# A hybrid attention / state-space block on one Trainium2 core: the first k tile of the normed input lies 384 bytes off and is multiplied first, and small tiles are placed further ahead

## The chip, the core and the metric

The kernel runs on one core of a Trainium2 chip. Its time is the device time of one execution in microseconds (us). TensorE (PE) multiplies matrices, with its weight loads shown apart (PEld); VectorE (DVE) and ScalarE (ACT) do the elementwise work, GpSimd (POOL) a little of it, and the SyncE queue (SP) issues the loads of the weights.

## The reference

Two layers (`DEPTH = 2`) over 256 tokens of width 1024, all in float32; what matters here is that nearly every step multiplies 256 tokens by a large weight matrix:

```python
for l in range(DEPTH):
    h = rms_norm(x, norm_mix_w[l])
    proj = h @ w_in                      # 1024 -> 9320 columns: q, k, v, index, z, xbc, dt, gates
    a = dsa_attention(q, k, v, qi, ki, wi)       # top-64 attention, two blocks of 128 queries
    b = mamba2_branch(z, xbc, dt, ...)           # causal conv, chunked scan, gated group norm
    x = x + (sigmoid(g_attn) * (a @ w_proj_attn) + sigmoid(g_ssd) * (b @ w_proj_ssd)) @ w_out
    h = rms_norm(x, norm_ffn_w[l])
    u = causal_dwconv(h @ w_up)                  # 1024 -> 2 * 2816
    x = x + (silu(u[:, :2816]) * u[:, 2816:]) @ w_down
return rms_norm(x, norm_final_w)
```

## The kernel before

**Products in three parts.** Each float32 operand is split into a high part (rounded to fp32r) and a low part (what is left). A product is summed from high x high, high x low and low x high, so each 128x128 weight tile costs three matmuls with 256 columns (the tokens). Activations lie feature-major: k tile `k` is `[128, 256]`, 1024 bytes per partition.

**Chunks.** Weights come in chunks of 512 KB (eight 128x128 tiles) through a ring of five `raw` tiles. `take()` hands out the next chunk: ScalarE casts it to `whi` (L199), VectorE subtracts to `wlo` (L200), three such pairs deep. Some chunks are split early, into activation tiles that are free for a while (names that begin with `e`: `es0`, `ez0`, `ex0`, ...); their loads go through the same ring and queues.

**Loops.** `n_outer` makes one output tile of 128 features from one to three chunks: in each chunk `feed_high` goes over the eight k tiles with high x high (L376) and high x low (L377), and `feed_low` then goes over them again with `wlo` (L382): 24 matmuls. `k_outer` keeps four output tiles open and goes over k outside, also 24 matmuls for each chunk. `wide` (L548, L551, L554) has the activation as stationary and the weights as moving operand, with 308 or 512 columns.

**Who reads what, for each layer.** The scaled normed input `hxh`/`hxl` (made by `Normed.scaled`) feeds 56 `n_outer` chunks in the mixer (24 of the convolved columns, 16 gates, 16 `z`) and 36 in the FFN's up projection. `aH`/`aL` (attention) feed 8, `bH`/`bL` (scan) 8 in `k_outer` and 8 in `n_outer`, `mH`/`mL` (merged) 4 and 4, and the unscaled parts `uh`/`ul` the first 8 of the FFN and all of `wide`. `fH`/`fL` (FFN hidden, 22 k tiles) feed 11 chunks in `k_outer` and 12 in `n_outer`: 528 matmuls a layer, of which 192 read the tiles `fH0`, `fL0`, `fH1`, `fL1`.

**Side work.** Attention, scan and norms run as generators that `take()` steps on, so small matmuls of theirs stand between, and inside, the chunks. The framework's scheduler sets each engine's final order; engines run their own in order.

**Places.** Tiles of a pool lie one behind another in the order in which they are first made; a tile with a tag takes over that tag's place. Counted modulo 512 bytes within a partition, as built: all `whi`/`wlo` 64; `hxh`, `hxl`, `mH`, `mL`, `aH`, `aL`, `fH2` to `fH5` and their low parts 0; `bH`, `fH0`, `fH1`, `fL0`, `fL1` 384; `bL`, `uh`, `ul` 64. One weight tile is 512 bytes per partition and one k tile 1024, so all tiles of an array share its figure.

Of the kernel before, what the change touches and what calls it, by code (L numbers as in the profile page):

```python
# [63 lines left out]
def hybrid_kernel(ctx: ExitStack, tc: tile.TileContext, a: dict, out: bass.AP):  # L64
# [104 lines left out]
    def load_some(until=None):  # L169
        while st["dma"] < len(order) and st["dma"] < (until or st["prep"] + RAW_BUFS):  # L170
# [132 lines left out]
    class Normed:  # L303


        def __init__(self, nw, split=True):
            self.nw = nw
            self.acc = tmp.tile([P, T], F32, name="ssq", tag="ssq", bufs=3)
            if split:
                self.h = [act.tile([P, 4, T], F32R, name=f"uh{i}", tag=t) for i, t in enumerate(("Bm", "Cm"))]  # L310
                self.l = [act.tile([P, 4, T], F32R, name=f"ul{i}", tag=t) for i, t in enumerate(("lg0", "lg1"))]
            else:
                self.xw = act.tile([P, KD, T], F32, name="xw", tag="hxh")
            self.split = split

        def hi(self, k):
# [28 lines left out]
                nc.scalar.activation(self.xw[:, k, :], x, AF.Copy, scale=self.nw[:, k:k + 1])  # L345

        def scaled(self):
            h = act.tile([P, KD, T], F32R, name="hxh", tag="hxh")
            l = act.tile([P, KD, T], F32R, name="hxl", tag="hxl")
            for k in range(KD):  # L350
                t = tmp.tile([P, T], F32, name="ht", tag="ct", bufs=3)
                nc.vector.scalar_tensor_tensor(t, xT[:, k, :], self.nw[:, k:k + 1], self.row, op0=OP.mult, op1=OP.mult)
                nc.scalar.copy(out=h[:, k, :], in_=t)
                nc.vector.tensor_sub(l[:, k, :], t, h[:, k, :].bitcast(F32))
            return (lambda k: h[:, k, :]), (lambda k: l[:, k, :])

        def factor(self):
            ps = pst("sb", [P, 2], 2)
# [37 lines left out]
    def n_outer(parts):  # L396

        ps = acc_tile()
        for i, (hi, lo, ks) in enumerate(parts):
            wh, wl = take()  # L400
            feed_high(ps, wh, hi, lo, ks, i == 0)
            feed_low(ps, wl, hi, ks, i == len(parts) - 1)
        return ps


    nrm = Normed(sm("nmw", 0))
    side("norm", nrm.factor(), KD + 1)

    for l in range(L):

        tok = [act.tile([P, 8 * T], F32, name=f"big{t}", tag=f"big{t}")[:, :1856] for t in range(2)]
        V = [act.tile([P, T], F32, name=f"V{t}", tag=f"V{t}") for t in range(2)]
        wd = act.tile([P, 2, 40], F32, name="wd", tag="wd")

        def rotate(v, t, heads, dim, rot, o):
            h = rot // 2
# [17 lines left out]
        def index_stage():  # L434

            for t in range(2):
                s = slice(t * P, (t + 1) * P)
                rotate(tok[t][:, 0:576], t, 9, 64, 16, 64)
                kd = tmp.tile([P, 2, 64], F32, name="kd", tag="kd", bufs=1)
                nc.vector.tensor_copy(kd, tok[t][:, 512:576][:, None, :].to_broadcast([P, 2, 64]))  # L440
                yield 1
                ps = pst("sa", [P, 4, P], 2)
                for i in range(4):
                    nc.tensor.transpose(ps[:, i, :], tok[t][:, i * P:(i + 1) * P], ident)
                nc.scalar.copy(out=qiT[:, :, s], in_=ps)
                ps = pst("sa", [P, P], 2)
                nc.tensor.transpose(ps, kd.rearrange("p a b -> p (a b)"), ident)
                nc.scalar.copy(out=kiT[:, s], in_=ps)
            for b in range(2):
                yield 1  # L450
                yield from choose(b)
# [48 lines left out]
        dA = act.tile([P, 2, 32], F32, name="dA", tag="dA")  # L500
        Pc = act.tile([P, 2, 32], F32, name="Pc", tag="Pc")
        nP = act.tile([P, 2, 32], F32, name="nP", tag="nP")
        dec = act.tile([P, 32], F32, name="dec", tag="dec")

        prd = dram.tile([32, 2, P], F32, name=f"prd{l}")

        def decay_stage():
            def f64(tag):
                return tmp.tile([P, 2, 32], F32, name=tag, tag=tag, bufs=1)

            xd, u, z, z2, pl = f64("xd"), f64("u"), f64("z"), f64("z2"), f64("pl")
            ea = tmp.tile([P, 32], F32, name="ea", tag="ea", bufs=1)
            nc.scalar.activation(ea, sm("alog", l), AF.Exp)
            nc.vector.tensor_add(xd, wd[:, :, 8:40], sm("dtb", l)[:, None, :].to_broadcast([P, 2, 32]))
            nc.vector.scalar_tensor_tensor(u, xd, -1.0, xd, op0=OP.mult, op1=OP.min)
            nc.scalar.activation(u, u, AF.Exp)
            nc.vector.tensor_scalar(z, u, 2.0, None, op0=OP.add)
            nc.vector.reciprocal(z, z)
            nc.vector.tensor_mul(z, z, u)
            nc.vector.tensor_mul(z2, z, z)  # L520
            nc.vector.tensor_scalar(pl, z2, 2.0 / 17, None, op0=OP.mult)
            for n in range(15, 1, -2):
                nc.vector.scalar_tensor_tensor(pl, pl, 2.0 / n, z2, op0=OP.add, op1=OP.mult)
# [310 lines left out]
            gate_and_project(n)  # L834


        mH = act.tile([P, KD, T], F32R, name="mH", tag="hxh")
        mL = act.tile([P, KD, T], F32R, name="mL", tag="hxl")
        bh = lambda k: bH[k // 4][:, k % 4, :]
        bl = lambda k: bL[k // 4][:, k % 4, :]  # L840
        def merge(n, ps):
# [78 lines left out]


    finish("norm")
    y = act.tile([P, 2, 2, 512], F32, name="y", tag="hxl")
    for c in range(2):
        for h in range(2):
            ps = pst("acc", [P, 512], 4)
# [93 lines left out]
```

## Time and profile before

| | |
|---|---|
| time, median of 3 runs (lowest to highest) | 1068.74 us (1068.19 to 1072.17) |
| profiled execution: its time, its span | 1067.94 us, 1066.1 us |
| PE busy | 1056.1 us, 99% of the span, 8713 matmuls |
| PEld busy | 1020.8 us, 96% |
| DVE, ACT, POOL busy | 860.7 us (81%), 694.8 us (65%), 81.4 us (8%) |
| HBM read | 189.26 MB, 179 GB/s over the span |

PE's busy time covers the span because matmuls overlap: one takes some 280 ns from its start to its end, and the next begins after 113 to 118 ns. So the busy share says nothing of how close together they come. That is read from the times at which matmuls start.

### The profile page before, as it was taken

The numbers are of one execution on the slowest core, as the hardware profiler recorded it, in microseconds if no ns is written. First come the engines' busy times: TensorE is split into PE (matmuls) and PEld (weight loads), VectorE is DVE, ScalarE is ACT, GpSimd is POOL, SyncE is SP. The second block draws the span as 40 slices with busy tenths as digits, with TensorE's granted clock in tenths as the row PEclk, the third lists the DMA queues.
The fourth block names the chain that finished last, engine by engine and source line by source line (L and its number), as shares of the span: only waits on it lengthen the run. The fifth ranks groups of instructions, "written<-read, shape, count | busy, mean of one in ns | idle before, by whom it ended". The sixth has DMA issues, their size and how long they took to land.

```text
span 1066.1 us, 22377 instructions
## 1 busy us (share of the span) xinstructions
PE 1056.1 (99%) x8713; PEld 1020.8 (96%) x8713; DVE 860.7 (81%) x1652; ACT 694.8 (65%) x1285; POOL 81.4 (8%) x88
## 2 busy tenths in 40 slices
PE   9999999999999999999999999999999999999997
PEld 8799999999999999999997999899999999999997
DVE  6999979789677898886577999887895878988643
ACT  6769878567555566665465789775674556666552
POOL 3000000033001000000100000000420020000011
PEclk9999999999999999999999999999999999999999
DMA  8655445555677256667645654554666761666661
GB/s 309 208 185 191 141 140 179 148 181 176 201 235 247 80 159 197 195 194 240 195 134 167 220 159 139 168 168 146 179 183 207 259 218 42 195 197 195 185 184 51
DMA packets 53688, 191.81 MB, mean 180 GB/s; under 512 B 6176, under 2 KB 7216, under 8 KB 52560
## 3 DMA queue, kind: packets, MB, share of 16 engines
q1 hardware_dynamic: 51840, 180.71, 54.5%
q0 software_dynamic: 1600, 9.69, 2.4%
q8 instruction: 68, 1.11, 0.4%
q14 instruction: 36, 0.29, 0.1%
q10 hardware_dynamic: 144, 0.01, 0.0%
HBM read 189.26 MB, written 1.11 MB: 179 GB/s over the span
## 4 chain that ended last, share of the span: by engine, by line
PE 87%; DMA 6%; DVE 3%; issue 1%; ACT 1%; POOL 0%; SPq 0%; POOLq 0%; DVEq 0%; ACTq 0%
PE acc L376 22%; PE acc L377 22%; PE acc L382 22%; DMA raw<-in_wu_dram 5%; PE acc L548 3%; PE acc L551 3%; PE acc L554 3%; PE sa L377 2%; PE sa L376 2%; PE sa L382 2%; PE sb L731 2%; DVE ul L330 1%; PE sa L615 1%; PE sa L640 1%; DVE wlo L200 1%
## 5 line engine op out<-in xcount | busy, mean ns | idle before, releaser
L199 ACT CAST whi<-raw 128x1024 fp32r<-128x1024 f32 (+2 forms) x320 | 332.0, 1040 | 225.2 <-PE acc L377 137.0
L200 DVE TENSOR_TENSOR wlo<-raw,whi 128x1024 fp32r<-128x1024 f32 (+2 forms) x320 | 386.5, 1210 | 102.1 <-ACT whi L199 95.4
L376 PE MATMUL acc<-hxh,whi 128*128 128x256 f32 x1456 | 352.3, 282 | 0.0
L377 PE MATMUL acc<-hxl,whi 128*128 128x256 f32 x1456 | 349.7, 280 | 0.0
L377 PEld LDWEIGHTS acc<-hxl,whi 128*128 128x128 f32 x1456 | 274.3, 188 | 1.8 <-issue 1.6
L376 PEld LDWEIGHTS acc<-hxh,whi 128*128 128x128 f32 x1456 | 274.3, 188 | 1.5 <-issue 1.2
L382 PE MATMUL acc<-hxh,wlo 128*128 128x256 f32 x1456 | 200.6, 279 | 0.0
L382 PEld LDWEIGHTS acc<-hxh,wlo 128*128 128x128 f32 x1456 | 182.0, 188 | 0.6 <-issue 0.5
L675 DVE SCALAR_TENSOR_TENSOR cv<-acc,half,cv 128x255 f32<-128x255 f32 (+2 forms) x144 | 66.6, 472 | 4.1 <-ACT cv L673 3.7
L877 DVE SCALAR_TENSOR_TENSOR cv<-acc,small,cv 128x255 f32<-128x255 f32 (+1 forms) x144 | 68.5, 477 | 1.3
L343 POOL TENSOR_TENSOR ssq<-ssq,sq 128x256 f32<-128x256 f32 x30 | 27.8, 928 | 498.4 <-ACT sq L339 495.1
L376 PE MATMUL acc<-fH,whi 128*128 128x256 f32 x264 | 64.0, 277 | 0.0
L377 PE MATMUL acc<-fL,whi 128*128 128x256 f32 x264 | 63.9, 277 | 0.0
L377 PEld LDWEIGHTS acc<-fL,whi 128*128 128x128 f32 x264 | 49.6, 188 | 0.0
L376 PEld LDWEIGHTS acc<-fH,whi 128*128 128x128 f32 x264 | 49.5, 188 | 0.0
L377 PE MATMUL acc<-bL,whi 128*128 128x256 f32 x192 | 47.6, 282 | 0.0
L376 PE MATMUL acc<-bH,whi 128*128 128x256 f32 x192 | 47.5, 279 | 0.0
L721 ACT ACTIVATE bc<-bc,nP 128x128 f32<-128x128 f32 x128 | 40.5, 392 | 7.5 <-DMA bc<-prd 7.4
L830 POOL TENSOR_TENSOR ssq<-ssq,sq 128x256 f32<-128x256 f32 x24 | 32.2, 1343 | 136.5 <-ACT sq L829 136.1
L875 ACT ACTIVATE cv<-acc,small 128x256 f32<-128x256 f32 x72 | 40.6, 563 | 0.1
L382 PE MATMUL acc<-fH,wlo 128*128 128x256 f32 x264 | 37.8, 277 | 0.0
L377 PEld LDWEIGHTS acc<-bL,whi 128*128 128x128 f32 x192 | 36.2, 188 | 0.0
(346 smaller groups left out, 2011.4 us busy)
## 6 DMA issues: line engine op xcount, KB each, us to landing
raw<-in_wu_dram SPq DMA_DIRECT2D x88, 512.0 KB, 4.0
raw<-in_wx_dram SPq DMA_DIRECT2D x48, 512.0 KB, 3.7
raw<-in_wd_dram SPq DMA_DIRECT2D x38, 512.0 KB, 3.7
raw<-in_wz_dram SPq DMA_DIRECT2D x32, 512.0 KB, 3.6
raw<-in_wp_dram SPq DMA_DIRECT2D x32, 512.0 KB, 4.4
raw<-in_wq_dram SPq DMA_DIRECT2D x24, 512.0 KB, 4.2
raw<-in_wgs_dram SPq DMA_DIRECT2D x16, 512.0 KB, 3.5
bc<-prd POOLq DMA_DIRECT2D x8, 1024.0 KB, 6.0
```

The costliest lines, as they stand in the source:

```text
L199: nc.scalar.copy(out=hi, in_=r)
L200: nc.vector.tensor_sub(lo, r, hi.bitcast(F32))
L376: nc.tensor.matmul(ps, wh[:, j, :], hi(k), start=first and j == 0, stop=False)
L377: nc.tensor.matmul(ps, wh[:, j, :], lo(k), start=False, stop=False)
L382: st["mm"] = nc.tensor.matmul(ps, wl[:, j, :], hi(k), start=False, stop=last and j == len(ks) - 1)
L548: nc.tensor.matmul(ps, hi[:, s], w[0], start=first, stop=False)
L551: nc.tensor.matmul(ps, lo[:, s], w[0], start=False, stop=False)
L675: nc.vector.scalar_tensor_tensor(v[:, j:], ps[:, :T - j], cw(l, 3 - j, i), v[:, j:], op0=OP.mult, op1=OP.add)
L721: nc.scalar.activation(E[:, h, :], E[:, h, :], AF.Relu, bias=nP[:, c, 8 * g + h:8 * g + h + 1])
L830: nc.gpsimd.tensor_add(acc, acc, sq)
L875: nc.scalar.activation(v, uu, AF.Identity, scale=fw(l, 2, i), bias=fb(l, i))
L877: nc.vector.scalar_tensor_tensor(v[:, j:], uu[:, :T - j], fw(l, 2 - j, i), v[:, j:], op0=OP.mult, op1=OP.add)
```

## The change

It does four things. The tiles `hxh` and `hxl` get 512 bytes more (`ROOM`), and `scaled` puts k tile 0 behind the others, at element 7 * 256 + 96, with k tiles 1 to 7 ahead of it from element 0 on. `n_outer` begins each chunk with the three matmuls of its first k tile (high x high, low x high, high x low) and then feeds the others as before; this holds for all its chunks, whatever they read. The small tiles `dec` and `wd` are made ahead of others, and some scratch tiles share tags (`kd` with `bt`; `xd`, `u`, `z`, `z2` as one tile with `cbm`), which makes the room and shifts what lies behind.

```diff
+SHIFT = 96
+ROOM = 128
...
+    def roomy(name, tag, dtype=F32R):
+        t = act.tile([P, KD * T + ROOM], dtype, name=name, tag=tag)
+        return t[:, :KD * T].rearrange("p (k t) -> p k t", k=KD)
...
         def scaled(self):
-            h = act.tile([P, KD, T], F32R, name="hxh", tag="hxh")
-            l = act.tile([P, KD, T], F32R, name="hxl", tag="hxl")
+            h, l = ([t[:, o:o + T] for o in [(KD - 1) * T + SHIFT] + [k * T for k in range(KD - 1)]]
+                    for t in (act.tile([P, KD * T + ROOM], F32R, name=n, tag=n) for n in ("hxh", "hxl")))
...
             wh, wl = take()
-            feed_high(ps, wh, hi, lo, ks, i == 0)
-            feed_low(ps, wl, hi, ks, i == len(parts) - 1)
+            k = ks[0]
+            nc.tensor.matmul(ps, wh[:, 0, :], hi(k), start=i == 0, stop=False)
+            nc.tensor.matmul(ps, wl[:, 0, :], hi(k), start=False, stop=False)
+            nc.tensor.matmul(ps, wh[:, 0, :], lo(k), start=False, stop=False)
+            feed_high(ps, wh[:, 1:], hi, lo, ks[1:], False)
+            feed_low(ps, wl[:, 1:], hi, ks[1:], i == len(parts) - 1)
...
+    dec = act.tile([P, 32], F32, name="dec")
...
+        wd = act.tile([P, 2, 40], F32, name="wd", tag="wd")
         tok = [...]
-        wd = act.tile([P, 2, 40], F32, name="wd", tag="wd")
...
-        dec = act.tile([P, 32], F32, name="dec", tag="dec")
...
-        mH = act.tile([P, KD, T], F32R, name="mH", tag="hxh")
-        mL = act.tile([P, KD, T], F32R, name="mL", tag="hxl")
+        mH, mL = roomy("mH", "hxh"), roomy("mL", "hxl")
```

Places modulo 512 bytes, as the two kernels are built:

| tile | before | changed |
|---|---|---|
| `whi`, `wlo` (all slots) | 64 | 64 |
| `hxh`, `hxl`: k tile 0 | 0 | 384 |
| `hxh`, `hxl`: k tiles 1 to 7; `mH`, `mL`, `aH`, `aL`, `fH2` to `fH5` and low parts | 0 | 0 |
| `bH`, `fH0`, `fH1`, `fL0`, `fL1`, early `es` | 384 | 0 |
| `bL`, early `ebig` | 64 | 0 |
| `uh`, `ul` | 64 | 192 |
| early `ez`, `ex`, `eths`, `eXt` | 0 | 0 |

**First place: TensorE, a chunk of the FFN's up projection.** Before (tile names carry a number for each use; `wlo` belongs to the `whi` numbered one lower):

```order
L377 MATMUL acc_5399<-hxl_4837,whi_5325 128x256
L382 MATMUL acc_5399<-hxh_4836,wlo_5326 128x256 x8
L376 MATMUL acc_5430<-hxh_4836,whi_5356 128x256
L377 MATMUL acc_5430<-hxl_4837,whi_5356 128x256
L376 MATMUL acc_5430<-hxh_4836,whi_5356 128x256
```

The same in the changed kernel, where L412 to L414 are the new lines and L386, L387, L392 what was L376, L377, L382:

```order
L387 MATMUL acc_5277<-hxl_4834,whi_5203 128x256
L392 MATMUL acc_5277<-hxh_4833,wlo_5204 128x256 x7
L412 MATMUL acc_5321<-hxh_4833,whi_5247 128x256
L413 MATMUL acc_5321<-hxh_4833,wlo_5248 128x256
L414 MATMUL acc_5321<-hxl_4834,whi_5247 128x256
L386 MATMUL acc_5321<-hxh_4833,whi_5247 128x256
L387 MATMUL acc_5321<-hxl_4834,whi_5247 128x256
```

One matmul with `wlo` has moved from behind the sixteen with `whi` to second place, and the first three matmuls read the k tile that lies off.

**Second place: TensorE, the scan branch's output projection by `n_outer`, where the second chunk of an output tile begins.** Before:

```order
L382 MATMUL acc_4169<-bH1_3307,wlo_4100 128x256 x4
L376 MATMUL acc_4169<-bH2_3489,whi_4135 128x256
L377 MATMUL acc_4169<-bL2_3490,whi_4135 128x256
...
L382 MATMUL acc_4169<-bH2_3489,wlo_4136 128x256 x4
L382 MATMUL acc_4169<-bH3_3656,wlo_4136 128x256 x4
L376 MATMUL acc_4240<-bH0_3124,whi_4170 128x256
```

Changed:

```order
L392 MATMUL acc_4166<-bH1_3304,wlo_4097 128x256 x4
L412 MATMUL acc_4166<-bH2_3486,whi_4132 128x256
L412 MATMUL acc_4237<-bH0_3121,whi_4167 128x256
L413 MATMUL acc_4166<-bH2_3486,wlo_4133 128x256
L414 MATMUL acc_4166<-bL2_3487,whi_4132 128x256
L386 MATMUL acc_4166<-bH2_3486,whi_4132 128x256
```

`wlo_4133` is asked for after the chunk's first matmul, and the scheduler has put the first matmul of the next chunk between. Layer 1 has the same at the same chunk.

**Third place: VectorE, what stands ahead of that `wlo`.** Before:

```order
L844 TENSOR_TENSOR mg0_2466<-mg0_2466,ths_863 128x256 x2
L200 TENSOR_TENSOR ex1_4177<-raw_4056,ex0_4176 128x1024
L846 TENSOR_TENSOR mL_3831<-mg0_2466,mH_3830 128x256 x2
L200 TENSOR_TENSOR wlo_4136<-raw_3996,whi_4135 128x1024
L846 TENSOR_TENSOR mL_3831<-mg0_2466,mH_3830 128x256 x2
```

Changed:

```order
L856 TENSOR_TENSOR mg0_2463<-mg0_2463,ths_860 128x256 x2
L210 TENSOR_TENSOR ex1_4174<-raw_4053,ex0_4173 128x1024
L858 TENSOR_TENSOR mL_3828<-mg0_2463,mH_3827 128x256 x2
L210 TENSOR_TENSOR wlo_4133<-raw_3993,whi_4132 128x1024
L858 TENSOR_TENSOR mL_3828<-mg0_2463,mH_3827 128x256 x2
```

Nothing has moved there: the subtraction stands behind the merge of the four tiles that `k_outer` made and behind an early chunk. SP's and POOL's orders are the same in both kernels; on VectorE and ScalarE some side work of the mixers moves by a few places.

## Rows read from the trace of the kernel before

**Rows 1.** The page's busy times, granted clock (tenths, 40 slices) and chain.

```profile
PE 1056.1 (99%) x8713; PEld 1020.8 (96%) x8713; DVE 860.7 (81%) x1652; ACT 694.8 (65%) x1285; POOL 81.4 (8%) x88
...
PEclk9999999999999999999999999999999999999999
...
PE 87%; DMA 6%; DVE 3%; issue 1%; ACT 1%; POOL 0%; SPq 0%; POOLq 0%; DVEq 0%; ACTq 0%
```

**Rows 2.** Timeline, PE, FFN up, layer 0: start and length (us), engine, line.

```profile
399.91 0.28 PE L376 MATMUL acc<-hxh,whi 128*128 128x256 f32 x1
...
421.67 0.28 PE L376 MATMUL acc<-hxh,whi 128*128 128x256 f32 x1
```

**Rows 3.** Timeline, PE, mixer and output projection of layer 0.

```profile
209.20 0.28 PE L376 MATMUL acc<-hxh,whi 128*128 128x256 f32 x1
...
223.34 0.28 PE L376 MATMUL acc<-hxh,whi 128*128 128x256 f32 x1
...
327.97 0.28 PE L376 MATMUL acc<-mH,whi 128*128 128x256 f32 x1
...
342.11 0.28 PE L376 MATMUL acc<-mH,whi 128*128 128x256 f32 x1
```

**Rows 4.** Timeline, PE, FFN down, layer 0.

```profile
470.63 0.28 PE L376 MATMUL acc<-fH,whi 128*128 128x256 f32 x1
...
481.94 0.28 PE L376 MATMUL acc<-fH,whi 128*128 128x256 f32 x1
...
500.98 0.28 PE L376 MATMUL acc<-fH,whi 128*128 128x256 f32 x1
...
503.81 0.28 PE L376 MATMUL acc<-fH,whi 128*128 128x256 f32 x1
...
505.63 0.28 PE L382 MATMUL acc<-fH,wlo 128*128 128x256 f32 x1
```

**Rows 5.** Timeline, PE, mixers: two of the merged rows of `feed_low`.

```profile
102.58 1.07 PE L382 MATMUL acc<-hxh,wlo 128*128 128x256 f32 x8
...
801.04 1.10 PE L382 MATMUL acc<-hxh,wlo 128*128 128x256 f32 x8
```

**Rows 6.** Timeline, PE, mixer of layer 0: side work inside a chunk.

```profile
126.88 1.03 PE L615 MATMUL sa<-kk,qT 128*128 128x256 f32 x4
```

**Rows 7.** Timeline, PE, scan branch's projection by `k_outer`, layer 0.

```profile
282.54 0.28 PE L376 MATMUL acc<-bH,whi 128*128 128x256 f32 x1
...
302.43 0.28 PE L376 MATMUL acc<-bH,whi 128*128 128x256 f32 x1
```

**Rows 8.** Timeline, DVE and PE: `wlo` made, and its chunk's first matmul.

```profile
310.45 1.22 DVE L200 TENSOR_TENSOR wlo<-raw,whi 128x1024 fp32r<-128x1024 f32 x1
...
310.95 0.28 PE L376 MATMUL acc<-bH,whi 128*128 128x256 f32 x1
...
344.85 1.21 DVE L200 TENSOR_TENSOR wlo<-raw,whi 128x1024 fp32r<-128x1024 f32 x1
...
344.93 0.28 PE L376 MATMUL acc<-mH,whi 128*128 128x256 f32 x1
...
834.94 1.22 DVE L200 TENSOR_TENSOR wlo<-raw,whi 128x1024 fp32r<-128x1024 f32 x1
...
836.05 0.28 PE L376 MATMUL acc<-bH,whi 128*128 128x256 f32 x1
...
869.68 1.21 DVE L200 TENSOR_TENSOR wlo<-raw,whi 128x1024 fp32r<-128x1024 f32 x1
...
870.03 0.28 PE L376 MATMUL acc<-mH,whi 128*128 128x256 f32 x1
```

**Rows 9.** Timeline, ACT; in brackets the idle time ahead and what ended it.

```profile
293.16 1.05 ACT L199 CAST whi<-raw 128x1024 fp32r<-128x1024 f32 x1 [1.78 <-PE sa L377]
...
307.55 1.05 ACT L199 CAST ex<-raw 128x1024 fp32r<-128x1024 f32 x1 [4.81 <-DMA raw<-in_wu_dram]
```

**Rows 10.** Groups by form: `wide` with 512 columns (busy, mean ns of one).

```profile
L548 PE MATMUL acc<-whi,uh 128*128 128x512 f32 x96 | 30.4, 395 | 0.0
```

More of the change, by code (lines that the diff above doesn't have):

```diff
@@ L180, in split_tiles @@
             t0, t1 = early[j]
+            if t0 in ("hxh", "hxl"):
+                t = roomy(f"e{t0}", t0).rearrange("p (a k) t -> p a (k t)", a=2)
+                return [t[:, 0], t[:, 1]]
             if t0 == t1:
@@ L312, in __init__ @@
             else:
-                self.xw = act.tile([P, KD, T], F32, name="xw", tag="hxh")
+                self.xw = roomy("xw", "hxh", F32)
             self.split = split
@@ L352, in scaled @@
                 nc.vector.scalar_tensor_tensor(t, xT[:, k, :], self.nw[:, k:k + 1], self.row, op0=OP.mult, op1=OP.mult)
-                nc.scalar.copy(out=h[:, k, :], in_=t)
-                nc.vector.tensor_sub(l[:, k, :], t, h[:, k, :].bitcast(F32))
-            return (lambda k: h[:, k, :]), (lambda k: l[:, k, :])
+                nc.scalar.copy(out=h[k], in_=t)
+                nc.vector.tensor_sub(l[k], t, h[k].bitcast(F32))
+            return (lambda k: h[k]), (lambda k: l[k])
         def factor(self):
@@ L438, in index_stage @@
                 rotate(tok[t][:, 0:576], t, 9, 64, 16, 64)
-                kd = tmp.tile([P, 2, 64], F32, name="kd", tag="kd", bufs=1)
+                kd = tmp.tile([P, 2, 64], F32, name="kd", tag="bt", bufs=1)
                 nc.vector.tensor_copy(kd, tok[t][:, 512:576][:, None, :].to_broadcast([P, 2, 64]))
@@ L502, in hybrid_kernel @@
         nP = act.tile([P, 2, 32], F32, name="nP", tag="nP")
-        dec = act.tile([P, 32], F32, name="dec", tag="dec")
         prd = dram.tile([32, 2, P], F32, name=f"prd{l}")
         def decay_stage():
-            def f64(tag):
-                return tmp.tile([P, 2, 32], F32, name=tag, tag=tag, bufs=1)
-            xd, u, z, z2, pl = f64("xd"), f64("u"), f64("z"), f64("z2"), f64("pl")
+            decays = tmp.tile([P, 4, 2, 32], F32, name="decays", tag="cbm", bufs=2)
+            xd, u, z, z2 = (decays[:, i] for i in range(4))
+            pl = tmp.tile([P, 2, 32], F32, name="pl", tag="pl", bufs=1)
             ea = tmp.tile([P, 32], F32, name="ea", tag="ea", bufs=1)
@@ L922, in hybrid_kernel @@
     finish("norm")
-    y = act.tile([P, 2, 2, 512], F32, name="y", tag="hxl")
+    y = roomy("y", "hxl", F32).rearrange("p (c h a) b -> p c h (a b)", c=2, h=2)
     for c in range(2):
```

## The prediction, made before the changed kernel ran

> **What bounds the kernel now.** I read the page first. PE is busy for 99% of the span at the full granted clock in every slice, and the chain that ended last is 87% PE [rows 1]; no other engine comes near. So the question is not who makes PE wait but how closely its matmuls follow each other. The page cannot tell that (each matmul's length overlaps the next), so I took start times from the timeline and divided.
>
> In the FFN's up projection, eight whole chunks (192 matmuls) take 421.67 - 399.91 = 21.76 us, 113.3 ns each [rows 2]. In the mixer, on the same tiles `hxh`/`hxl` and the same kind of weights, five chunks (120 matmuls) take 14.14 us, 117.8 ns each, and so do five chunks on `mH`/`mL` [rows 3]. I call these the short and the long spacing. Nobody waits in either. A whole run of eight low matmuls shows which one holds: 1.07 us or about 1.10 [rows 5]. Of the 93 such runs on `hxh` in the two mixers, 28 are short and 65 longer; in layer 0's FFN 35 whole runs of 36 are short. Going through the timeline, the spacing on these tiles changes only where other work stands between, as four attention matmuls do inside a chunk at 126.88 us [rows 6]; otherwise it stays for dozens of chunks. It is a lock, not a load.
>
> The FFN's down projection shows what sets the lock. While `fH0` to `fL1` are read (384 bytes modulo 512), 96 matmuls take 481.94 - 470.63 = 11.31 us: 117.8 ns, from the first on, although the chunk before ran short. From `fH2` on (0 modulo 512) the next 168 take 19.04 us: 113.3 [rows 4]. Weights, shapes, loop and engines are the same; only the place of the moving operand differs. The same return happens ten times in each direction over both layers (once in `k_outer`, four times in `n_outer`, per layer), always to the short spacing. After it, 16 matmuls from 503.81 take 1.82 us, 7 ns over 16 short ones: that is the price of the return [rows 4]. So reading a tile at 384 costs 4.5 ns per matmul and then puts the following tiles at 0 into the short lock, while tiles at 0 keep whichever lock they entered with.
>
> [...]
>
> **The change, part by part** (against the profiled execution's own 1067.94 us: span 1066.1 and 1.8 around it; the median of the three runs is 0.8 higher).
>
> 1. *Chunks on `hxh`/`hxl`.* Each of the 184 now begins with three matmuls at 384 and goes on at 0: 3 x 4.5 + 7 = 20 ns over a short chunk. A long chunk costs 24 x 4.5 = 108 ns over it. In the mixers 112 chunks, 65/93 of them long, 78: these gain 88 ns each, -6.9 us. The 34 short ones and the FFNs' 72 lose 20 ns each, +2.1. But about half of the mixers' chunks are cut by side work as in rows 6, and behind a cut the lock is drawn anew: 56 chunks x 12 matmuls x 4.5 ns x 0.7 = +2.1. Together -2.7 us. That three matmuls are enough to reach the state from which the return starts is my reading of 470.63, where the long spacing holds at once; the trace has no stay shorter than 24.
> 2. *`aH`/`aL`*, 16 chunks, each right behind a healed one: 16 x 0.7 x 108 ns = 1.2, less relapses: -0.7.
> 3. *`bH`/`bL`* move from 384 and 64 to 0. Now 168 matmuls take 19.89 us, 118.4 ns [rows 7]. They follow short chunks, so 768 x 5.1 ns = -3.9 us if they enter short and keep it; if they enter long, -0.5.
> 4. *`mH`/`mL`* stay at 0, and are long now only because `bH`/`bL` are: 384 x 4.5 = -1.7, or 0.
> 5. *`fH0` to `fL1`* move to 0: 384 x 4.5 = -1.7, and ten returns are saved: -1.8. They lose the healing at 384: should the FFN's end leave them long, all 1056 would be, 1056 x 4.5 - 1.8 = +2.9.
> 6. *`uh`/`ul`* at 192: in the FFN's first eight chunks of each layer, 384 matmuls in all, mostly long now, bounds -1.7 and +1.7 (one step of 4.5 ns either way); I take -0.3, as an unchanged lock. In `wide` they are stationary; 512 columns, 3 x 96 matmuls [rows 10], at +-4.5 ns: +-1.3; I take 0.
> 7. *`wlo` is wanted 14 matmuls earlier*, at the second of a chunk instead of the seventeenth. Mostly it is ready microseconds ahead. Four chunks are not so lucky [rows 8]: in layer 0 it is done at 310.45 + 1.22 = 311.67 where the second matmul now stands at 310.95 + 0.11 = 311.06: 0.6 us late; at 346.06 against 345.04: 1.0; in layer 1 at 836.16 against 836.16: 0; at 870.89 against 870.14: 0.75. What is ahead of it there does not hang on PE: ScalarE is last released by PE at 293.16 and then held up 4.81 us by the load of an early chunk [rows 9], with VectorE in order behind it. So where parts 3 and 4 make PE earlier, the wait grows: (310.95 - 293.16) x 5.1/118.4 = 0.8 us at the first, estimated 0.5 at each of the other three. Sum 2.35 + 2.3 = +4.6 us. Behind PE's wait stand all chunks that follow. The matmul that the scheduler puts between hides 0.1 of it and asks for a `whi` whose cast ends no earlier.
> 8. After such a wait the lock is drawn again for the rest of `bH` and `mH`: +0.5.
> 9. Shared scratch tiles, `dec` without a tag, larger tiles: their owners are a whole stage or layer apart, no instruction is added on VectorE, ScalarE or the queues: 0. Side work moved by a few places in the mixers: within +-1.
>
> Sum: -2.7 - 0.7 - 3.9 - 1.7 - 1.8 - 0.3 + 4.6 + 0.5 = -6.0, so 1061.9 us; I say **1062**.
>
> **The rivals.**
> - *The feed eats more* (0.12). If the early loads bind from 293 to 347 us and again in layer 1, parts 3, 4 and 8 return nothing and the 2.35 us of part 7 remain: -2.7 - 0.7 - 1.8 - 0.3 + 2.35 = -3.2, 1064.8. For it: ScalarE's wait for a load in rows 9. Against: PE itself waits nowhere there now.
> - *The down projection locks long* (0.11): parts 3 to 5 at their bad bounds, -0.5, 0 and +2.9, part 7 at its 2.35: -2.7 - 0.7 - 0.5 + 2.9 - 0.3 + 2.35 = +1, 1069. For it: half the draws after a cut come out long. Against: its chunks follow 36 short ones without a cut.
> - *Placement does nothing* (0.06): the two spacings have another cause than the place of the tiles, the locks are drawn as before, and only part 7's 2.35 us come on top: 1070.3. Rows 4 speak against it. [...]
> - *The short stay at 384 lands the tiles at 0 in the long lock* (0.08), the side on which it gets slower. Place: the fourth matmul of each of the 184 chunks. Then the 34 + 72 short chunks become long, 106 x 108 ns = +11.4; `aH` +0.5; parts 3 to 5 at their bad bounds, +2.4; part 7, +2.35: +16.7, 1084.6. It decides the sign when more than about a third of the stays end so (6.0/16.7 and the lost gain). For it: no stay of three is seen. Against: all ten exits go the other way.
>
> **How the numbers follow.** The forecast has 0.63; its own range is 1058 to 1066, from the bounds of parts 6, 7 and 9 and of the relapses. A difference of 0.5%, 5.3 us, is about what a measurement of this kernel can tell from none. Below 1063.4 lies some three quarters of the forecast's share, 0.47, and nearly nothing of the rivals: faster 0.48. Slower by 0.5%, over 1074, is the last rival and little else: 0.09. The rest, 0.43, is the forecast's upper part and the three rivals between. The range of 1057 to 1070 leaves out the last rival and about a tenth more.
>
> **What would show it.** In the changed profile the low runs of the FFN's up projection, now seven matmuls, should take 0.96 us (6 x 113.3 + 280 ns) in both layers, and in the mixers nearly all of them too, wherever no side work cuts the chunk; the first three starts of a chunk 117 to 118 ns apart, the next two or three 117 to 114, then 113. `bH`, `mH` and `fH0` should run at 113.3 up to the first wait. PE should wait, between first and second matmul, for VectorE's `wlo` at four chunks, 0.5 to 1.5 us each. I am wrong if the spacing behind the third matmul stays at 117.8, if the output projections are long, or if a wait for `wlo` turns up in the mixers, where it costs PE time that I hold to be free.

## The result: slower by 0.9%, and the profile after

| | before | changed |
|---|---|---|
| time, median of 4 runs each (lowest to highest) | 1069.41 us (1068.19 to 1072.17) | 1079.19 us (1078.50 to 1080.36) |
| ratio, 95% interval | | 1.0089 (1.0066 to 1.0111) |
| profiled execution: its time, its span | 1067.94 us, 1066.1 us | 1079.55 us, 1077.7 us |

The forecast was 1062.0 us and a range of 1057 to 1070. It was wrong in sign: 9.8 us slower by the medians, 11.6 by the spans.

The page of the changed kernel answers to [rows 1]. PE is as busy as it was and its granted clock as full, so again nothing is learned from shares; only PE's part of the chain grew, from 87 to 91%.

```profile
PE 1062.6 (99%) x8713; PEld 1024.9 (95%) x8713; DVE 862.0 (80%) x1652; ACT 693.0 (64%) x1285; POOL 82.2 (8%) x88
...
PEclk9999999999999999999999999999999999999999
...
PE 91%; DMA 4%; DVE 2%; ACT 1%; issue 1%; SPq 0%; POOL 0%; POOLq 0%; ACTq 0%; DVEq 0%
```

The FFN's up projection, PE's timeline, answers to [rows 2] and [rows 5]: two chunk starts eight chunks apart, and one low run between them.

```profile
399.13 0.28 PE L412 MATMUL acc<-hxh,whi 128*128 128x256 f32 x1
...
401.13 0.99 PE L392 MATMUL acc<-hxh,wlo 128*128 128x256 f32 x7
...
421.74 0.28 PE L412 MATMUL acc<-hxh,whi 128*128 128x256 f32 x1
```

192 matmuls take 421.74 - 399.13 = 22.61 us, 117.8 ns each, where they took 113.3. Seven low matmuls take 0.99 us and not the 0.96 that I gave as the sign. This holds in all 72 chunks of both layers. The down projection after it, answering to [rows 4], is long too, and no longer turns short at `fH2`:

```profile
475.45 0.28 PE L386 MATMUL acc<-fH,whi 128*128 128x256 f32 x1
...
486.76 0.28 PE L386 MATMUL acc<-fH,whi 128*128 128x256 f32 x1
...
506.54 0.28 PE L412 MATMUL acc<-fH,whi 128*128 128x256 f32 x1
```

The first 96 take 11.31 us as before; the next 168, now all at 0 modulo 512 as well, take 19.78 us, 117.7 ns, against 19.04.

The groups by form show both signs at once (busy us, mean ns of one). Where the matmuls run at the short spacing their mean length is 276 to 277 ns here, at the long one 281. `fH` went from 277 to 281; `bH` from 279 to 276 and `mH` from 281 to 276, as forecast. `wide`, [rows 10], went from 395 to 399.

```profile
L386 PE MATMUL acc<-fH,whi 128*128 128x256 f32 x240 | 59.6, 281 | 0.0
...
L386 PE MATMUL acc<-bH,whi 128*128 128x256 f32 x176 | 42.3, 276 | 0.0
...
L561 PE MATMUL acc<-whi,uh 128*128 128x512 f32 x96 | 30.8, 399 | 0.0
...
L386 PE MATMUL acc<-mH,whi 128*128 128x256 f32 x88 | 21.2, 276 | 0.0
```

PE's waits (line waited for: us, times, longest). Those for the split weights, lines L209 and L210, are new but for 0.3 us; the 1.3 us for the norm's `ssq` and `sq` that stood there before are gone.

```profile
PE acc L413 <- DVE wlo L210: 3.6, 4, 1.2
PE acc L412 <- ACT whi L209: 2.7, 3, 1.1
PE sb L235 <- DVE ones L223: 1.3, 1, 1.3
PE acc L561 <- ACT ebig L209: 0.3, 1, 0.3
```

The timeline shows waits for `whi` and `wlo`, answering to [rows 8], and two early loads that hold up ScalarE, answering to [rows 9]. The first three rows stand at the first `n_outer` chunk of `bH` in layer 0:

```profile
300.77 1.05 ACT L209 CAST ez<-raw 128x1024 fp32r<-128x1024 f32 x1 [6.50 <-DMA raw<-in_wu_dram]
...
302.81 0.38 PE L412 MATMUL acc<-bH,whi 128*128 128x256 f32 x1 [0.75 <-ACT whi L209]
...
304.26 0.39 PE L413 MATMUL acc<-bH,wlo 128*128 128x256 f32 x1 [1.07 <-DVE wlo L210]
...
309.38 1.05 ACT L209 CAST ex<-raw 128x1024 fp32r<-128x1024 f32 x1 [4.73 <-DMA raw<-in_wu_dram]
...
346.36 1.21 DVE L210 TENSOR_TENSOR wlo<-raw,whi 128x1024 fp32r<-128x1024 f32 x1
...
347.62 0.38 PE L413 MATMUL acc<-mH,wlo 128*128 128x256 f32 x1 [1.08 <-DVE wlo L210]
```

To see where 11.6 us went I added up, from the trace's start times, what each spacing exceeds 113.3 ns, in us over both layers; spacings over 125 ns stand apart.

| matmuls on | before | changed | difference |
|---|---|---|---|
| `hxh`/`hxl`, FFN | 0.04 | 7.67 | +7.63 |
| `hxh`/`hxl`, mixers | 8.23 | 7.37 | -0.86 |
| `aH`/`aL` | 1.11 | 0.66 | -0.45 |
| `bH`/`bL` | 2.96 | 0.06 | -2.90 |
| `mH`/`mL` | 1.72 | 0.05 | -1.67 |
| `fH`/`fL` | 1.78 | 4.70 | +2.92 |
| `uh`/`ul` | 1.52 | 0.49 | -1.03 |
| over 125 ns, on `bH` and `mH` | 0.88 | 8.36 | +7.48 |
| over 125 ns, on `uh` | 2.36 | 0.68 | -1.68 |
| over 125 ns, others | 11.35 | 11.55 | +0.20 |
| the two stretches of `wide` (start to first `hxh` chunk; end of layer 0's FFN to first `hxh` chunk) | 60.0, 54.1 | 61.2, 54.9 | +2.0 |

The differences add up to +11.6, the difference of the spans.

Spacings over 125 ns follow an interruption or a wait, with one exception: the 0.88 us before on `bH` and `mH` are 62 steps of 127 or 128 ns in which PE goes from `bL` (64 modulo 512) back to `bH` (384) and waits for nothing, as from 283.37 to 283.50 us in the kernel before:

```profile
283.37 0.29 PE L377 MATMUL sa<-bL,whi 128*128 128x256 f32 x1
283.50 0.28 PE L376 MATMUL acc<-bH,whi 128*128 128x256 f32 x1
283.61 0.28 PE L377 MATMUL acc<-bL,whi 128*128 128x256 f32 x1
```

In the changed kernel both lie at 0, no such step is left, and the whole 8.36 us are waits. So by place `bH` gained 3.8 us, and the waits grew by 8.4.

### The profile page after: what moved, and what is told of

Its sections match the earlier page's. It is cut to its first block, busy times and chain, and to the rows that moved or that the text cites. A ratio compares the mean times of both kernels' runs of the same rounds, so it can differ in the third digit from the quotient of the medians.

```text
span 1077.7 us, 22385 instructions
## 1 busy us (share of the span) xinstructions
PE 1062.6 (99%) x8713; PEld 1024.9 (95%) x8713; DVE 862.0 (80%) x1652; ACT 693.0 (64%) x1285; POOL 82.2 (8%) x88
## 3 DMA queue, kind: packets, MB, share of 16 engines
q8 instruction: 68, 1.11, 0.4%
HBM read 189.26 MB, written 1.11 MB: 177 GB/s over the span
## 4 chain that ended last, share of the span: by engine, by line
PE 91%; DMA 4%; DVE 2%; ACT 1%; issue 1%; SPq 0%; POOL 0%; POOLq 0%; ACTq 0%; DVEq 0%
PE acc L386 20%; PE acc L387 20%; PE acc L392 20%; DMA raw<-in_wu_dram 3%; PE acc L413 3%; PE acc L412 3%; PE acc L414 3%; PE acc L561 3%; PE acc L567 3%; PE acc L564 3%; PE sa L387 2%; PE sa L386 2%; PE sa L392 2%; PE sb L744 2%; PE sa L628 1%; PE sa L653 1%
## 5 line engine op out<-in xcount | busy, mean ns | idle before, releaser
L209 ACT CAST whi<-raw 128x1024 fp32r<-128x1024 f32 (+2 forms) x320 | 331.3, 1039 | 220.8 <-PE acc L387 133.2
L210 DVE TENSOR_TENSOR wlo<-raw,whi 128x1024 fp32r<-128x1024 f32 (+2 forms) x320 | 387.3, 1213 | 106.7 <-ACT whi L209 100.4
L386 PE MATMUL acc<-hxh,whi 128*128 128x256 f32 x1274 | 309.6, 281 | 0.0
L387 PE MATMUL acc<-hxl,whi 128*128 128x256 f32 x1274 | 309.4, 281 | 0.0
L387 PEld LDWEIGHTS acc<-hxl,whi 128*128 128x128 f32 x1274 | 240.3, 189 | 0.6 <-issue 0.5
L386 PEld LDWEIGHTS acc<-hxh,whi 128*128 128x128 f32 x1274 | 240.0, 188 | 0.2 <-issue 0.2
L392 PE MATMUL acc<-hxh,wlo 128*128 128x256 f32 x1274 | 180.5, 281 | 0.0
L392 PEld LDWEIGHTS acc<-hxh,wlo 128*128 128x128 f32 x1274 | 162.7, 189 | 0.8 <-issue 0.7
L387 PE MATMUL acc<-fL,whi 128*128 128x256 f32 x240 | 59.6, 281 | 0.0
L386 PE MATMUL acc<-fH,whi 128*128 128x256 f32 x240 | 59.6, 281 | 0.0
L412 PE MATMUL acc<-hxh,whi 128*128 128x256 f32 x182 | 54.2, 298 | 0.0
L413 PE MATMUL acc<-hxh,wlo 128*128 128x256 f32 x182 | 51.6, 283 | 0.0
L414 PE MATMUL acc<-hxl,whi 128*128 128x256 f32 x182 | 51.3, 282 | 0.0
L386 PEld LDWEIGHTS acc<-fH,whi 128*128 128x128 f32 x240 | 45.5, 189 | 0.0
L387 PEld LDWEIGHTS acc<-fL,whi 128*128 128x128 f32 x240 | 45.3, 189 | 0.0
L386 PE MATMUL acc<-bH,whi 128*128 128x256 f32 x176 | 42.3, 276 | 0.0
L387 PE MATMUL acc<-bL,whi 128*128 128x256 f32 x176 | 42.3, 276 | 0.0
```

What stands on the lines that cost most here:

```text
L209: nc.scalar.copy(out=hi, in_=r)
L210: nc.vector.tensor_sub(lo, r, hi.bitcast(F32))
L386: nc.tensor.matmul(ps, wh[:, j, :], hi(k), start=first and j == 0, stop=False)
L387: nc.tensor.matmul(ps, wh[:, j, :], lo(k), start=False, stop=False)
L392: st["mm"] = nc.tensor.matmul(ps, wl[:, j, :], hi(k), start=False, stop=last and j == len(ks) - 1)
L412: nc.tensor.matmul(ps, wh[:, 0, :], hi(k), start=i == 0, stop=False)
```

## The experiments

The kernel before ran beside each group; its median there was 1068.0 (e1 to e4), 1068.5 (e5 to e7), 1068.9 (e8 to e10) and 1068.5 us (e11, e12).

| run | what | median us | ratio to before (95%) |
|---|---|---|---|
| e1 | changed, `SHIFT = 0` | 1082.0 | 1.0125 (1.0107 to 1.0143) |
| e2 | changed, old order | 1081.8 | 1.0126 (1.0107 to 1.0144) |
| e3 | moved tiles alone | 1079.1 | 1.0108 (1.0086 to 1.0130) |
| e4 | new order alone | 1070.8 | 1.0023 (1.0009 to 1.0037) |
| e6 | changed, `uh` at 64 | 1076.8 | 1.0060 (1.0026 to 1.0094) |
| e7 | moved tiles, `uh` at 64 | 1079.9 | 1.0097 (1.0076 to 1.0118) |
| e9 | changed, `SHIFT = 16` | 1068.2 | 0.9988 (0.9974 to 1.0002) |
| e10 | e9, new order on `hxh` alone | 1067.5 | 0.9982 (0.9962 to 1.0002) |
| e11 | e9, new order on `hxh`, `mH`, `uh`; `uh` at 64 | 1064.7 | 0.9955 (0.9939 to 0.9972) |
| e12 | e7, `es` and `bH` at 384 | 1068.8 | 1.0014 (0.9993 to 1.0036) |

**Which of the three parts costs it: e1 to e4.** My first theory was the rival of the forecast that came nearest, that three matmuls at 384 leave the tiles at 0 in the long lock.

```diff
# e1, of the changed kernel
-SHIFT = 96
+SHIFT = 0
# e2, of the changed kernel; e3: this and SHIFT = 0; e4: the reverse of this, in the kernel before
-            k = ks[0]
-            nc.tensor.matmul(ps, wh[:, 0, :], hi(k), start=i == 0, stop=False)
...
-            feed_low(ps, wl[:, 1:], hi, ks[1:], i == len(parts) - 1)
+            feed_high(ps, wh, hi, lo, ks, i == 0)
+            feed_low(ps, wl, hi, ks, i == len(parts) - 1)
```

> The changed kernel with SHIFT = 0: the first k tile still lies behind the others and is still multiplied first, three matmuls at once, but at 0 modulo 512 like the rest. Theory 'stay' (three matmuls at 384 leave the tiles behind them in the long lock): the FFN's chunks on hxh run at 113.3 ns again (-7.6 us over both layers against the changed kernel) and hand the down projection the short lock (-2.9), the waits for wlo stay: 1079.2 - 10.5 = 1068.7 us, 1066 to 1071. Rival 'order' (the new order of the first three matmuls throws the lock, wherever the tile lies): the FFN stays at 117.8 and the time at 1079, 1077 to 1081.

> The changed kernel with n_outer's old order: the first k tile lies at 384, and is read twice at the start of a chunk and once at the start of its low run. Theory 'stay': stays of two and of one also leave the tiles at 0 long, so the FFN and the down projection stay long, and only the waits for wlo go (6.3 us in the changed kernel's chain of waits, against about 2 with the old order): about 1075 us, 1072 to 1077. Rival 'order': FFN and down projection short, mixers too: 1060 to 1065. If a stay of one heals and a stay of two does not, the low runs of a chunk are short and the high ones long: between the two, about 1070.

> Only the moved tiles: the old order and SHIFT = 0, so bH, bL, fH0, fL0, fH1, fL1 come to 0 modulo 512 and uh, ul to 192, nothing else. Theories 'stay' and 'order' alike: hxh in the FFN short as in the kernel before, bH and mH short (2.9 and 1.7 us), no returns at fH2 (1.8), uh near short (1.0): 1069.4 - 7.4 = 1062.0 us, 1059 to 1066, with the mixers' draws as the spread. Rival 'places' (the moved tiles cost the time, through the scratch tiles that share a place or through a down projection that locks long): 1069 or more.

> The kernel before with only n_outer's new order, all tiles where they were. Theory 'stay': hxh lies at 0 throughout, the FFN stays short; PE waits for wlo at the first chunks of the two late projections, 2 to 4 us in all, and those waits draw the mixers' locks anew: 1069.4 + 3 = 1072 us, 1070 to 1075. Rival 'order': the FFN's chunks on hxh go long, +7.6, and with the waits 1079 to 1082.

e1 and e3 settle it against that theory. In e3 there is neither a tile of `hxh` at 384 nor a new order, and the FFN is long all the same. Its low runs of eight, PE's timeline:

```profile
403.15 1.11 PE L392 MATMUL acc<-hxh,wlo 128*128 128x256 f32 x8
...
405.98 1.11 PE L392 MATMUL acc<-hxh,wlo 128*128 128x256 f32 x8
```

A chunk takes 405.98 - 403.15 = 2.83 us, 117.9 ns each. So the moved tiles alone cost about what the whole change does (+11.1 us), though `hxh` does not move. The order alone costs 2.8, within the range of 'stay' for e4. By the medians a shifted tile costs 2.7 more in the old order (e2 against e3) and saves about 3 in the new one (the changed kernel against e1); the intervals overlap in both pairs, so neither is clear of noise. The time of e2 fits none of its three theories, that of e1 lies just above its rival's range.

**What a tile's place does by itself: e5, and the entry into the FFN: e6, e7.** What changes for `hxh` in e3 is what is read ahead of it. The nearest are `uh` and `ul`: they stand at 192, no longer 64, because `dec` (128 bytes) is made before them.

```diff
# e6, of the changed kernel; e7, of e3
-    dec = act.tile([P, 32], F32, name="dec")
     nrm = Normed(sm("nmw", 0))
+    dec = act.tile([P, 32], F32, name="dec")
```

> A kernel of its own that computes nothing of the reference: 6960 matmuls of 256 columns on PE alone, weights at 64 modulo 512, moving tiles at chosen places, no other engine at work. It sets a lock (24 matmuls at 384, then 24 at 0; or 24 at 192, then 24 at 0), then reads some place for 1 to 24 matmuls and goes back to 0 for 24. Theory 'handover' (the place that was read before decides the spacing at 0, which then holds): behind 24 at 384 and at 64 the tiles at 0 run at 113.3 ns, behind 24 at 192 at 117.8, and chunks whose first three matmuls stand at 384 run short when entered short and long when entered long. Theory 'stay' (three at 384 always leave 117.8): long from either entry. Rival 'load' (the spacings come from the other engines' reads and writes): one spacing everywhere at 0, whatever came before.

> The changed kernel with dec made behind the first uh and ul instead of ahead of them: these four tiles lie at 64 modulo 512 as before the change, all else stays (SHIFT, the order, the other tiles). Theory 'handover': the FFN's chunks on hxh enter short and stay so but for 20 ns a chunk (-7.7 + 1.4), the down projection is short (-4.7), uh itself long (+1.0): 1079.2 - 10 = 1069 us, 1066 to 1072. Theory 'stay': the FFN stays long whatever it is entered from, 1080 us, 1078 to 1082.

> As the run with only the moved tiles (old order, SHIFT = 0), but dec behind uh and ul, which lie at 64 again. Theory 'handover': FFN short (-7.7), down projection short throughout (-4.7), uh long (+1.0), bH and mH as the aH chunks leave them: 1079.1 - 11.4 = 1067.7 us, 1061 (bH and mH short too) to 1069. Rival 'another of the moved tiles': 1079 as without this edit.

e5 shows both spacings, and the passage between them, on PE alone at a granted clock of 1.000: the rival "load" is out. 24 matmuls at 0 run at 113.3 or 117.8, whichever lock they are in; at 64 they settle at 120.0 (119.2 in the mean of 24 from the short lock), at 192 at 118.7. It also shows that a place does not hand on one lock. The trace's spacings in ns, consecutive matmuls, the bar where the place changes:

```
0 (short) | 24 at 384: ... 118 118 118 117 | at 0: 117 116 114 113 113 114 113   short again
0 (short) |  1 at 384: 119                 | at 0: 114 118 118 117 118 118 118   long, for all 24
0 (long)  | 24 at 384: 118 118 120 118 ... | at 0: 114 118 118 117 118 118 118   long, for all 24
0 (long, from 192) | 24 at 384: 122 118 117 118 ... | at 0: 117 116 114 113 114   short
0 (short) | 24 at 192: 122 120 119 115 ... | at 0: 118 119 118 118 117 118 118   long, for all 24
```

The second line is long after one matmul; the third enters 384 from such a state and comes back to it; the fourth enters from another long state, the one that 24 at 192 leave behind, and comes back short. Both states run at 117.8 and look alike until the place changes.

e6 fitted neither number: its 12 executions lie from 1066.6 to 1082.3 us. Its profiled one shows how that can be. In layer 0 the FFN's second chunk turns short and stays so, in layer 1 all are long, in one execution of one program. Two low runs of each layer:

```profile
400.68 0.96 PE L392 MATMUL acc<-hxh,wlo 128*128 128x256 f32 x7
403.42 0.96 PE L392 MATMUL acc<-hxh,wlo 128*128 128x256 f32 x7
...
910.15 0.99 PE L392 MATMUL acc<-hxh,wlo 128*128 128x256 f32 x7
912.97 0.99 PE L392 MATMUL acc<-hxh,wlo 128*128 128x256 f32 x7
```

So a stay of three at 384 can come back short (layer 0) and can come back long (layer 1). e7 was a plain miss: with `uh` at 64 the FFN stayed long (in layer 0 a low run every 2.83 us, 117.9 ns a matmul). The hand-over theory as I had put it, a place decides, fell; what was left of it is that a state does which the spacing does not tell, as e5's two at 117.8 ns show.

**Three states: e8, and the shift that leaves each of them: e9, e10.**

> Again a kernel that computes nothing of the reference: 6050 matmuls on PE alone. It sets one of three states: short; 'long A' (24 matmuls at 192, back to 0); 'long X' (one matmul at 384 out of the short state, back to 0). Then three chunks in the new order, with k tile 0 at some place (32 to 224, 384). Theory 'three states' (the long spacing has two hidden forms; from A a stay at 384 comes back short, from X it comes back in X; a stay at 64 comes back short from each within two chunks): 384 heals S and A and leaves X at 117.8 in all three chunks, 64 ends at 113.3 from all. Rival 'two states': X and A behave alike, and 384 heals both as in the run before. Cuts of 1 to 8 matmuls with 128 columns draw a state; behind them two chunks with 64 all end short, with 384 some stay long.

> The changed kernel with SHIFT = 16 for 96: k tile 0 of hxh and hxl lies at 64 modulo 512 in place of 384, all else as changed. Theory 'three states': every chunk on hxh comes back short at 20 ns a chunk, from the second on at the latest: FFN 7.7 to 1.5 (-6.2), down projection short (-4.7), mixers -1 to -3: 1079.2 - 12.9 = 1066.3 us, 1063 to 1070, the waits for wlo as they are. Rival 'the kernel's other traffic decides': the FFN stays long, 1077 to 1081. Rival 'only the entry counts' (as with uh at 64): spread over 1066 to 1082 from execution to execution.

> As the run with SHIFT = 16, and the new order only for the chunks on hxh: the chunks on aH, bH, mH, uh and fH go back to the old order, so wlo is wanted as late as before at the late projections. Theory 'three states': 3 to 6 us of waits for wlo and whi at bH and mH go (8.4 us of stalls there in the changed kernel), bH and mH keep the short lock that the healed chunks hand on: 1066.3 - 5 = 1061 us, 1058 to 1064. If aH hands the long lock to bH and mH, they run long (+5.1): 1066.

```diff
# e9, of the changed kernel
-SHIFT = 96
+SHIFT = 16
# e10, of e9: n_outer(parts, ahead=False), ahead set by the calls on hxh/hxl
+            if not ahead:
+                feed_high(ps, wh, hi, lo, ks, i == 0)
+                feed_low(ps, wl, hi, ks, i == len(parts) - 1)
+                continue
```

e8, PE's timeline: low runs of successive chunks, one chunk apart; a row takes in the next chunk's first two matmuls where a chunk follows. X with 64, then X with 384:

```profile
310.66 1.19 PE L120 MATMUL acc<-mh,wt 128*128 128x256 f32 x9
313.40 1.19 PE L120 MATMUL acc<-mh,wt 128*128 128x256 f32 x9
316.14 1.07 PE L120 MATMUL acc<-mh,wt 128*128 128x256 f32 x8
...
411.85 1.22 PE L120 MATMUL acc<-mh,wt 128*128 128x256 f32 x9
414.68 1.23 PE L120 MATMUL acc<-mh,wt 128*128 128x256 f32 x9
417.51 1.10 PE L120 MATMUL acc<-mh,wt 128*128 128x256 f32 x8
```

2.74 us a chunk (114.2 ns each, 20 ns over a short chunk) with 64; 2.83 (117.9) with 384, in all three chunks that were tried. From A and from S, 384 gives 2.74 as well. The steps of the changed kernel's FFN, from its second chunk on, are those of X with 384, of e9's first chunk those of X with 64 (spacings in ns; the first three follow the starts of the three matmuls of k tile 0):

```
e8, X, three at 384          118 119 120 | 116 115 119 117 118 118 118 117
changed kernel, 379.3 us     118 119 120 | 116 115 119 117 118 118 118 117
e8, X, three at 64           113 119 120 | 121 122 116 114 113 113 114 113
e9, first chunk, 373.1 us    112 119 120 | 121 122 116 114 113 113 114 113
```

Of 32 to 224 in steps of 32, three matmuls at 64, 96, 160, 192 and 224 ended short (113.3 ns) in e8 from all three states within two chunks; 128 did as 384, and 32 ended long (117.8) from all three, from the short one too. Of eight cuts by 128-column matmuls two drew X; 64 came back to 113.3 ns from both, 384 from neither. All this holds for stays of three. Other lengths at 384 do otherwise in e5: eight matmuls out of X come back short (118 119 120 117 118 118 117 118, then 117 115 115 113 at 0), four out of A come back long (121 118 117 119, then 114 118 118 117).

In e9 the FFN is short but for the 20 ns, and the 11 us are gone:

```profile
402.48 0.96 PE L392 MATMUL acc<-hxh,wlo 128*128 128x256 f32 x7
405.22 0.96 PE L392 MATMUL acc<-hxh,wlo 128*128 128x256 f32 x7
```

Excess over 113.3 ns, as in the table above: FFN 7.67 to 1.46, `fH` 4.70 to 0.04, mixers 7.37 to 6.18. The mixers gave 1.2, within what was expected.

e10 missed by 6 us (its second guess, 1066, came near the time, but `bH` and `mH` did not run long). `bH` lost its waits (first to last matmul 46.3 to 44.1 us, mean of both layers), but `uh` got them (23.2 to 25.0): PE now waits for the norm of the residual, `ssq`, which in e9 was ready.

```profile
PE sb L371 <- POOL ssq L353: 2.5, 2, 1.3
...
PE acc L392 <- DVE wlo L210: 1.1, 2, 0.6
```

**A version made from what was learned: e11; and what set the FFN's entry: e12.**

```diff
# e11, of e10: ahead also for the chunks on mH and uh; dec behind uh and ul, as in e6
# e12, of e7: 384 bytes ahead of the tiles s0 to s3, 128 behind them
+        act.tile([P, 96], F32, name="gap0", tag="gap0")
         qiT = act.tile([P, 4, T], F32, name="qiT", tag="s0")
         ...
+        act.tile([P, 32], F32, name="gap1", tag="gap1")
         bias = [act.tile([P, (b + 1) * P], F32, name=f"bias{b}", tag=f"bias{b}") for b in range(2)]
```

> SHIFT = 16 and the new order for the chunks on hxh, mH and uh, not on aH, bH and fH; dec behind uh and ul, which lie at 64. Against the run with the new order on hxh alone (1067.5 us): bH keeps its 44 us, the stretches of mH and uh together take 46.5 us instead of 48.0 in each layer (-1.5 each, as in the run with the new order everywhere), wide in layer 1 54.1 instead of 54.9 (-0.8): 1063.7 us, 1062 to 1066. Rival 'the early loads and the norms set that time, whatever PE saves': what is gained in one stretch is waited for in the next, 1067 to 1068.

> Only the moved tiles (old order, SHIFT = 0), with uh and ul back at 64 and, by two gaps, bH0 to bH3, the early weights es0 to es3 that share their places, fH0, fH1, fL0 and fL1 back at 384 modulo 512. Theory 'hand-over': the state in which uh is read in its last chunks decides the FFN's lock; with es at 384 the cuts in uh draw what they drew in the kernel before, so the FFN on hxh is short again (-7.7) and the down projection returns at fH2 as before (4.7 to 1.8 over short): 1079.9 - 10.6 = 1069 us, 1067 to 1072. Rival 'the places of bL, ebig or the scratch tiles': 1077 to 1081 as without this edit.

e11 measured 1064.7, inside its range, and is the one version that is faster than the kernel before, by 0.45% (0.3 to 0.6%). The rival had 1067 to 1068. But the trace does not show the gain where it was forecast. `wide`'s stretch in layer 1 is 54.1 us again, while `mH` and `uh` together still take 48.1 and 48.0 us, as in e10, and not 46.5: the wait for `ssq` is down to 0.3 us, and in its place PE waits for `wlo`.

```profile
PE acc L417 <- DVE wlo L210: 3.5, 4, 1.2
...
PE sb L371 <- POOL ssq L353: 0.3, 1, 0.3
```

That is the rival's mechanism. The profiled execution took 1066.5 us, as e10's did, and lies near the slow end of e11's (1062.9 to 1067.1); no trace shows where the faster ones gain.

In e12 the FFN is short: 2.72 us from low run to low run, 1.07 us each, in both layers, and the time is inside its range.

```profile
400.88 1.07 PE L392 MATMUL acc<-hxh,wlo 128*128 128x256 f32 x8
403.60 1.07 PE L392 MATMUL acc<-hxh,wlo 128*128 128x256 f32 x8
```

So with `uh` at 64 the FFN's lock hung on the places of the `s0` to `s3` tiles: in layer 0 a chunk takes 2.83 us in e7 and 2.72 in e12. They hold the early weights `es0` to `es3` of the FFN's first two chunks, `bH`, and tiles of the attention (`qiT`, `kk4`, `qT`), all of them read some 17 us or more ahead of `hxh`.

e8 shows the last link. With weights at 0, as those of `uh`'s last six chunks are, 24 matmuls at 64 hand on the long lock from S and X and the short one from A. At 192, where `uh` lies in the changed kernel, they hand on the long one from all three; from A and X they run short themselves and leave X behind. The kernels' traces show the same steps (spacings in ns; the bar stands where `uh`, or its place in e8, ends):

```
e8, A, 24 at 192          113 114 113 113 118 | 114 118 118 117 119   long
e3, layer 0, uh at 192    113 114 113 113 118 | 114 118 118 117 119   long
e8, X, 24 at 64           119 117 118 118 115 | 117 117 118 118 118   long
e7, layer 0, uh at 64     118 117 118 118 115 | 117 118 117 118 118   long
e8, A, 24 at 64           118 118 117 118 117 | 121 116 114 114 113   short
before, layer 0, uh at 64 118 117 119 117 118 | 123 118 114 113 113   short
```

With `uh` at 192, in both layers of the changed kernel, e1, e2 and e3, `uh` ends short and `hxh` begins long. With `uh` at 64, in both layers of the kernel before, e4 and e12, `uh` ends long and `hxh` begins short. The last low run of `uh` in layer 0, before and changed:

```profile
371.75 1.10 PE L382 MATMUL acc<-uh,epT 128*128 128x256 f32 x8
...
372.89 0.96 PE L392 MATMUL acc<-uh,epT 128*128 128x256 f32 x7
```

So by e8 and these steps the moved `uh` is enough for the long lock, and by e7 the moved `s` tiles are too; no run has `uh` at 192 with the `s` tiles at 384. That `es` matters through the state that the cuts in `uh` draw fits the traces of e7 and e12: behind the last cut the spacings on `uh` are 113 122 118 118 in e7's layer 0, 118 113 114 113 in its layer 1, and 124 118 117 118 and 123 118 118 117 in e12's two layers, and only behind these last two is `hxh` short. But no run sets `es` apart from `bH`'s own place or that of the attention's tiles.

## Why the prediction was wrong, step by step

**What the locks are: the step that failed.** "Reading a tile at 384 costs 4.5 ns per matmul and then puts the following tiles at 0 into the short lock, while tiles at 0 keep whichever lock they entered with." The first half was read from ten returns to short in [rows 4]. All ten had entered 384 from the short lock ("although the chunk before ran short"): they showed that it comes back, not that it heals. e5 and e8 show at least three states, two of them at 117.8 ns: three matmuls at 384 return short from S and A, and X to X. `uh` at 192 hands the changed kernel's FFN the state X, step for step as in e8, and its 72 chunks stay there, at 117.8 ns. A lone 113.3 or 117.8 told the spacing and not the state.

**Parts 1 and 2, -2.7 and -0.7.** The FFN's chunks were to lose 20 ns each, 1.4 us; they lost 7.6. That price is right for a stay that starts short (2.74 us a chunk in e8). The mixers gave 0.9 instead of 4.1, `aH` 0.5. (The count of 28 short runs in 93 is 30 in 101 over the whole trace, the same share.)

**Parts 3 and 4, -3.9 and -1.7.** Right: `bH` and `mH` entered short. `mH` gave 1.7, and `bH` 3.8: 2.9 in the row up to 125 ns, 0.9 in the steps from `bL` to `bH`, which the 118.4 ns of [rows 7] rightly held. In e3, with neither the stays nor the new order, `bH` and `mH` run long (3.4 and 1.7 us over 113.3 ns); in e1, with the order alone, `bH` is still 2.1 over. So the short entry came with the stays of three.

**Part 5, -1.8.** It came out at its bad bound to the digit, +2.9, and by the mechanism given: without 384 nothing turns `fH` short when the FFN hands on the long lock.

**Part 6, -0.3 for `uh` and 0 for `wide`.** `uh` gave 1.0. "As an unchanged lock" was the second error behind the result: what `uh` hands to `hxh` was never priced, and in the changed kernel it was the 7.6 and the 2.9. `wide` cost 2.0 against bounds of +-1.3: the 0.8 in layer 1 is there in the runs with `uh` at 192 and absent (54.1 us) in e4, e6, e7, e11 and e12 with 64. The 1.2 in layer 0 stays open: that stretch takes anything from 60.2 to 63.0 us in the traces of e1 to e12, at either place of `uh`.

**Parts 7 and 8, +4.6 and +0.5.** The four chunks of [rows 8] cost 5.3 us of waits, a little over the 4.6; in the two on `bH` PE waits for the `whi` of the matmul that stands between, in the two on `mH` for `wlo`. The sum had nothing for another 2.9 us at the first `n_outer` chunk of `bH` (in layer 0 behind an early load, `ez`, that held ScalarE up for 6.5 us). 1.7 us that were waited for at `uh` before went: +6.7 in all. That the new order costs, 2.8 us, is what e4 shows alone; part 8's draws came out short, 0.

**Part 9, 0.** The shared scratch tiles, which e12 keeps, cost nothing that it could show (ratio 1.0014). But I counted the moved early weights as nothing, since no instruction changed. With `uh` back at 64, their place, or that of the other `s` tiles, kept the FFN long all the same: e7 against e12.

**The rivals.** The last one, 0.08, had the sign, and 1084.6 against 1079.2, but not the mechanism: e3 has the loss without the stay. By its own terms a quarter of the stays would decide the sign (6.0 of 6.0 + 16.7), not a third. "Placement does nothing" is out by e5 and e8: on PE alone the spacing runs from 113.3 to 120.0 ns by the place of the moving tile (e5), and with that at 64 or 192 the place of the weights changes it too: at 64 it is 120.0 ns with weights at 64 and 113.3 or 117.8, by the state, with weights at 0 (e8). Why the places count, no run shows. "The feed eats more" came true in e10, where what `bH` saved was waited for at `uh`.

## What to carry to other kernels

Where a stream can lock at either of two rates, here 113.3 and 117.8 ns, a trace that shows it leaving a place at one rate proves nothing until the same exit has been seen from the other: find the rows that *entered* badly. A tile of 128 bytes that is made earlier moves what lies behind it (`dec` moved `uh` from 64 to 192), so a change of places is checked by listing, for each stretch, what was read just ahead, with its place and its weights' place. If executions of one program spread far wider than those of the others (e6), look for such a state being drawn anew before averaging.

## What the runs showed of the hardware

In e5, with weights at 64 modulo 512 and 256 columns, the steady spacing was 113.3 or 117.8 ns with the moving tile at 0, 120.0 at 64, 116.8 (mean of 24) at 96 and 118.7 at 192, and 256 bytes further on, at 256, 320, 352 and 448, the same. The place of the weights counted as well: with weights at 0, e8's matmuls at 64 and at 192 settled at 113.3 to 113.4 or at 117.8 ns, by the state they entered in, where with weights at 64 those of e5 took 120.0 and 118.7. Both ran on PE alone, at a granted clock of 1.000 (e5) and 0.999 (e8). In the traces of the kernel before and of the changed one, no stretch of 24 chunk matmuls, all with 256 columns and each with its own weight load, was under 113.3 ns a matmul.

One matmul at 384 behind a short stretch set the next 24 at 0 to 117.6 ns in the mean, which is 24 x 4.3 = 103 ns for a single matmul at another place; it did so each of the ten times that e8 tried it.
